# A two-layer decoder trunk on one core: TensorE's instructions in program order, paired values together

## The chip, the cores and the metric

The kernel runs on one core of one Trainium2 chip. The core has TensorE for matrix products (PE in the rows, and PEld for its weight loads), VectorE (DVE), ScalarE (ACT), GpSimd (POOL), and DMA queues that SyncE (SP) feeds. The metric is device time in microseconds, the median of several executions. One execution was profiled.

## The reference

Two layers work on x of 256 tokens and 1024 features in float32, with 256 tokens of memory. Each layer adds four parts to x:

```python
for layer in range(DEPTH):
    x = x + 0.5 * swiglu_ffn(rms_norm(x, ffn1_norm[layer]), ffn1_w_gu[layer], ffn1_w_down[layer])
    h = rms_norm(x, mix_norm[layer])
    if layer % 2 == 0:
        x = x + even_mixer(h, ...)      # sliding-window heads with sinks | stick-breaking heads
    else:
        x = x + odd_mixer(h, ...)       # 16 heads, a mixture of three dilated windows
    x = x + memory_cross_attention(rms_norm(x, xa_norm[layer]), rms_norm(mem, xa_mem_norm[layer]), ...)
    x = x + 0.5 * swiglu_ffn(rms_norm(x, ffn2_norm[layer]), ffn2_w_gu[layer], ffn2_w_down[layer])
```

The feed-forward has 2816 hidden features and is (silu(gate) * up) @ w_down. In the even mixer, 8 query heads share 2 key heads over a window of 128 tokens, and 8 more heads weigh by stick-breaking: the weight of a key is the exponential of log_sigmoid(z) plus the sum of log_sigmoid(-z) over the keys that come after it. Cross-attention has 4 heads of 256 features into the memory.

## The kernel before

Tokens are worked in two blocks t of 128. Each float32 product is made of three of a faster 32-bit type: a weight chunk is loaded (L170), rounded to a high half wh by ScalarE (L172), and the rest, wl, is made by VectorE (L174); activations are split in the same way (L187, L188). `mm3` (L179 to L181) then multiplies high by high, high by low and low by high into one PSUM bank. Feed-forwards use a wider form (L316, L317). Six PSUM banks named mm hold products, two named tp hold transpositions (L205, four blocks of 128 each, or L383). Ten work tiles wk, four raw buffers and ten weight pairs go round.

The order of the work around attention is written by a small planner in the kernel. `later(delay, fn, tag)` puts a step on a heap; each matmul group calls `tick(ns)`, which moves a made-up clock and runs a step that is due; `need(tag)` runs the rest of a tag at once. The delays stand in the table LAG. So the steps of attention are called between the matmuls of a projection. What is then issued first is not settled by that order alone: the framework's scheduler, on leaving the kernel, orders each engine's instructions by its own estimate of when they can start, and may pass a later one ahead. In a block under `tc.manual_schedule` an engine keeps the program's order; before, only the start of the first feed-forward (`start`) stands in one.

Both windowed attentions use `attend`. `one(i)` asks for scores of a head group (L594 in the even mixer, L827 in the odd one, each call for two groups at once), adds the bias (L601, L832), takes the maximum (L607, L837) and the exponential (L452). `share` divides by the sum (L438). `two` transposes the weights (L205), copies them to a work tile (L467) and asks for `values`, whose matmuls are on L482 by way of `value_pairs`. There are six groups in the even mixer's band part and twelve in the odd mixer.

The stick-breaking part (`stick`, from L680 on) makes scores for two heads at once (L691, L694), adds a mask (L699), takes an absolute value, an exponential and a logarithm on ScalarE (L702 to L704), and for each head VectorE and ScalarE make the high and low half of the log terms (L708, L710, L711). `after` sums them by three matmuls (L720, L721, L722), VectorE adds (L724), ScalarE takes the exponential (L725), and for every second head `values` follows. Beside it run the memory's keys (`mem.keys`, mm3, with squares on L511 and a scaling on L438).

In cross-attention, `attend` has its own form; its weights' transposition is asked for by `later(LAG['x_p'], turn, "o0")`.

Of the kernel before, what the change touches and what calls it, by code (L numbers as in the profile page):

```python
# [27 lines left out]


LAG = {  # L30
    "norm": 5000, "silu": 5000, "pv": 3000, "head256": 2200, "band": 7500, "band_gap": 2600, "band_p": 7500,
    "put": 400, "att_norm": 4500, "band_norm": 3500, "stick_gap": 1900, "stick_u": 3200, "stick_v": 1000, "stick_o": 1300, "head64": 7000,
    "att_first": 3800, "att_gap": 3300, "att_p": 17600, "att_o": 1800, "x_s": 18000, "x_p": 4000, "x_out": 3600,
    "mem_e": 5400, "mem_o": 4600, "rs64": 2700, "rs256": 1900, "rsband": 6100,
}

# [2 lines left out]
def kernel(  # L39
# [52 lines left out]
    def later(delay, fn, tag=None):  # L92
        serial[0] += 1
        heapq.heappush(heap, (clock[0] + delay, serial[0], tag, fn))
# [21 lines left out]
    plan = []  # L116
    for layer in range(DEPTH):
        plan += [(layer, 0, ffn1_norm), (layer, 1, mix_norm), (layer, 2, xa_norm), (layer, 3, ffn2_norm)]
    if phases is not None:
        plan = [plan[i] for i in phases]  # L120
# [30 lines left out]
    def slot(dt=F32):  # L151
        return big.tile([P, 1024], dt, name="big")

    def work(dt=F32):
        return wk.tile([P, 512], dt, name="wk")
# [30 lines left out]
    def split_to(dh, dl, src):  # L186
        nc.scalar.copy(dh, src)  # L187
        nc.vector.tensor_tensor(dl, src, f32(dh), op=ALU.subtract)  # L188
# [12 lines left out]
    def transpose4(src):  # L201

        ps = psum() if upcoming.get("starting") else tps()
        for b in range(4):
            nc.tensor.transpose(ps[:, b * P:(b + 1) * P], src[:, b * P:(b + 1) * P], ident)  # L205
        tick(440)
        return ps
# [51 lines left out]
    def project(view, lhs, evac, nk=NK, tags=(None, None)):  # L259

        head = nk - 8
        ps = [[None, None], [None, None]]

        def step(t, c, k, w):
            if k == 0:
                ps[t][c] = psum()
            mm3(ps[t][c], lhs(t, k), cols(w, c * 512, 512), k == 0, k == nk - 1)
            tick(650)

        for k in range(head):  # L270
            w = weights(view(k))
            for t in range(2):
                for c in range(2):
                    step(t, c, k, w)
        if tags[0]:
            need(tags[0])
        ws = []
        for k in range(head, nk):
            ws.append(weights(view(k)))
            for c in range(2):  # L280
                step(0, c, k, ws[-1])
        for c in range(2):
            evac(0, c, ps[0][c])
        if tags[1]:
            need(tags[1])
        for c in range(2):
            for k in range(head, nk):
                step(1, c, k, ws[k - head])
            evac(1, c, ps[1][c])
# [139 lines left out]
    def scale_heads(dst, src, r, n, pair=False):  # L429

        h = src.shape[1] // n
        if pair:
            nc.vector.tensor_tensor(
                dst.rearrange("p (b hf d) -> p hf b d", hf=2, d=n), src.rearrange("p (hf b d) -> p hf b d", hf=2, d=n),
                r[:, 0:h].rearrange("p (hf b) -> p hf b", hf=2).unsqueeze(3).broadcast_to([P, 2, h // 2, n]),
                op=ALU.mult)
        else:
            nc.vector.tensor_tensor(blocks(dst, n), blocks(src, n),  # L438
                                    r[:, 0:h].unsqueeze(2).broadcast_to([P, h, n]), op=ALU.mult)

    def attend(groups, scores, values, gap, norm, wait, first=0.0, tag=None, ready=None):

        def one(i):
            p, nm, sink = scores(groups[i])
            n, keys = p.shape[1], p.shape[2]
            dn = sm.tile([P, 4], F32, name="dn")  # L450
            for j in range(n):
                nc.scalar.activation(p[:, j, :], p[:, j, :], AF.Exp, bias=nm[:, j:j + 1], accum_out=dn[:, j:j + 1])  # L452
            p = p.rearrange("p a b -> p (a b)")
            if sink is not None:
                nc.scalar.activation(sink, sink, AF.Exp)

            def share():
                if sink is not None:
                    nc.vector.tensor_tensor(dn[:, 0:n], dn[:, 0:n], sink, op=ALU.add)
                nc.vector.reciprocal(dn[:, 0:n], dn[:, 0:n])  # L460
                scale_heads(p, p, dn, keys)
            later(norm, share, tag)

            def two():
                ps = transpose4(p)
                pt = work()
                nc.vector.tensor_copy(pt, ps)  # L467
                if ready is None:
                    later(LAG['pv'], lambda: values(groups[i], pt), tag)
                else:  # L470
                    ready(groups[i], lambda: later(LAG['pv'], lambda: values(groups[i], pt), tag))
            later(wait, two, tag)
            if i + 1 < len(groups):
                later(gap, lambda: one(i + 1), tag)
        later(first, lambda: one(0), tag)
# [395 lines left out]
    class Memory:  # L871
# [11 lines left out]
        def values(self, arrived):  # L883

            self.v = [(slot(F32R), slot(F32R)) for _ in range(2)]

            def evac(t, c, ps):
                split_to(*[d[:, c * 512:(c + 1) * 512] for d in self.v[t]], ps)
                if t == 1:
                    arrived(c)  # L890
            project(lambda k: self.w[k * P:(k + 1) * P, 1024:2048], self.parts, evac)

    def cross_attention(w_q, q_gain, k_gain, w_o, next_vec, mem):
# [55 lines left out]
        def evac(t, c, ps):  # L949
            norm_turn(t, c, ps)  # L950
            if c == 1:
                later(LAG['x_s'], lambda: attend(t, 0), "o0")
                later(LAG['x_s'] + 2000, lambda: attend(t, 1), "o0")
# [12 lines left out]
    neg_ur = const.tile([P, P], F32R, name="neg_ur")  # L966
    nc.vector.tensor_copy(neg_ur, neg_u)
    mems = [Memory(xa_w_kv[layer], xa_mem_norm[layer]) for layer in range(DEPTH)]
    for i, (layer, part, _) in enumerate(plan):
        j = layer // 2  # L970
        nxt = plan[i + 1][2][plan[i + 1][0]] if i + 1 < len(plan) else None
        mem = mems[layer]
        cross = (layer, 2) in [p[:2] for p in plan]
        if part == 0:
            ffn(ffn1_w_gu[layer], ffn1_w_down[layer], nxt, first=i == 0)
        elif part == 1 and layer % 2 == 0:
            even_mixer(ev_w_in[j], ev_q_gain[j], ev_k_gain[j], ev_sinks[j], ev_w_out[j], nxt, mem, first=i == 0)
        elif part == 1:
            odd_mixer(od_w_in[j], od_q_gain[j], od_k_gain[j], od_w_out[j], nxt, mem)
        elif part == 2:  # L980
            cross_attention(xa_w_q[layer], xa_q_gain[layer], xa_k_gain[layer], xa_w_o[layer], nxt, mem)
        else:
            ffn(ffn2_w_gu[layer], ffn2_w_down[layer], nxt)


def shape_constants():
# [53 lines left out]
```

## Time and profile before

| what | value |
|---|---|
| median of 3 runs | 1205.25 us (1201.16, 1205.25, 1205.61) |
| the profiled execution's own time | 1201.73 us |
| its span, first to last instruction | 1200.0 us |
| mean granted TensorE clock | 0.999 |
| TensorE busy | 1186.6 us, 99% of the span |
| TensorE weight loads busy | 997.0 us, 83% |
| VectorE busy | 774.3 us, 65% |
| ScalarE busy | 646.7 us, 54% |

A matmul's record lasts longer than the distance to the next one, so its busy time overlaps; distances between starts tell how fast the stream runs. The clock is given in shares of full speed.

### The profile page before, as it was taken

Reading aid. Unit: us, or ns where it says so; the run is one execution under the profiler, and the core shown is the slowest. Engines: PE = TensorE matmul, PEld = TensorE weight load, DVE = VectorE, ACT = ScalarE, POOL = GpSimd, SP = SyncE. Lnnn points to the kernel's source line nnn. Section 1 sums busy time; section 2 is a strip of 40 time slices with the busy share of each in tenths; the row PEclk is TensorE's granted clock in tenths of the full one; section 3 lists DMA queues with packets and bytes.
Section 4 is the critical chain, followed back from the end, with each engine's and each line's share of the span. In section 5 each row is a group of like instructions: output and inputs, shape, how many; then the busy total and the mean of one; then the engine's idle time right before and its main releaser. Section 6 shows DMA issues by size and latency. Waiting matters only on the chain.

```text
span 1200.0 us, 16955 instructions
## 1 busy us (share of the span) xinstructions
PE 1186.6 (99%) x6318; PEld 997.0 (83%) x6318; DVE 774.3 (65%) x1024; ACT 646.7 (54%) x1080; POOL 64.6 (5%) x123
## 2 busy tenths in 40 slices
PE   8999999999999999999999999999999999999998
PEld 6888888986788888888888888888777888888887
DVE  6766645696777666665375665376786676667651
ACT  6656534655665466555365564265763554655540
POOL 1000000200110000000000000032000100000000
PEclk9999999999999999999999999999999999999999
DMA  8865664731454485556385657445743645665550
GB/s 269 248 208 175 213 212 136 257 103 49 141 179 151 145 268 171 184 211 210 106 259 180 195 188 271 135 158 171 244 148 124 212 140 158 203 205 188 183 191 35
DMA packets 136756, 216.70 MB, mean 181 GB/s; under 512 B 10337, under 2 KB 104161, under 8 KB 136674
## 3 DMA queue, kind: packets, MB, share of 16 engines
q1 hardware_dynamic: 136674, 215.63, 55.1%
q8 instruction: 49, 0.80, 0.3%
q14 instruction: 33, 0.27, 0.1%
HBM read 214.54 MB, written 1.05 MB: 180 GB/s over the span
## 4 chain that ended last, share of the span: by engine, by line
PE 93%; DVE 3%; DMA 1%; ACT 1%; issue 1%; POOL 0%; SPq 0%; ACTq 0%; POOLq 0%; DVEq 0%
PE mm L316 23%; PE mm L179 18%; PE mm L181 18%; PE mm L180 18%; PE mm L317 12%; PE tp L205 3%; DVE wl L174 1%; PE mm L482 1%; DMA raw<-in_xa_w_o_dram 1%; PE mm L827 0%; PE mm L298 0%; DMA x<-in_x_dram 0%; ACT wh L172 0%; DVE big L188 0%; DMA raw<-in_ffn_w_gu_dram 0%
## 5 line engine op out<-in xcount | busy, mean ns | idle before, releaser
L174 DVE TENSOR_TENSOR wl<-raw,wh 128x1024 fp32r<-128x1024 f32 x386 | 463.8, 1220 | 144.7 <-ACT wh L172 142.5
L172 ACT CAST wh<-raw 128x1024 fp32r<-128x1024 f32 x386 | 394.2, 1051 | 156.0 <-PE mm L181 80.4
L316 PE MATMUL mm<-xs,wh 128*128 128x512 f32 x1184 | 413.7, 394 | 0.0
L317 PE MATMUL mm<-xs,wl 128*128 128x256 f32 x1184 | 331.8, 280 | 0.0
L316 PEld LDWEIGHTS mm<-xs,wh 128*128 128x128 f32 x1184 | 221.8, 187 | 50.4
L317 PEld LDWEIGHTS mm<-xs,wl 128*128 128x128 f32 x1184 | 223.8, 189 | 0.0
L179 PE MATMUL mm<-wh,big 128*128 128x512 f32 x480 | 191.5, 399 | 0.3 <-DVE wk L699 0.3
L180 PE MATMUL mm<-wl,big 128*128 128x512 f32 x480 | 188.3, 392 | 0.0
L181 PE MATMUL mm<-wh,big 128*128 128x512 f32 x480 | 188.3, 392 | 0.0
L179 PE MATMUL mm<-wh,xs 128*128 128x512 f32 (+1 forms) x432 | 171.8, 398 | 0.0
L181 PE MATMUL mm<-wh,xs 128*128 128x512 f32 (+1 forms) x432 | 167.1, 387 | 0.0
L180 PE MATMUL mm<-wl,xs 128*128 128x512 f32 (+1 forms) x432 | 167.0, 387 | 0.0
L320 ACT COPY wk<-mm 128x256 f32<-128x256 f32 x148 | 55.3, 374 | 147.7 <-PE mm L317 147.3
L321 DVE TENSOR_TENSOR wk<-mm,wk 128x256 f32<-128x256 f32 x148 | 62.2, 421 | 95.4 <-ACT wk L320 95.4
L179 PEld LDWEIGHTS mm<-wh,big 128*128 128x128 f32 x480 | 90.5, 188 | 20.1 <-issue 2.5
L181 PEld LDWEIGHTS mm<-wh,big 128*128 128x128 f32 x480 | 90.5, 189 | 19.5 <-issue 0.3
L180 PEld LDWEIGHTS mm<-wl,big 128*128 128x128 f32 x480 | 90.6, 189 | 17.5 <-issue 0.2
L181 PEld LDWEIGHTS mm<-wh,xs 128*128 128x128 f32 x432 | 81.1, 188 | 16.9 <-issue 0.2
L179 PEld LDWEIGHTS mm<-wh,xs 128*128 128x128 f32 x432 | 81.3, 188 | 15.0 <-issue 0.5
L180 PEld LDWEIGHTS mm<-wl,xs 128*128 128x128 f32 x432 | 81.4, 189 | 14.5 <-issue 0.2
L205 PE MATMUL tp<-ident,wk 128*128 128x128 f32 x352 | 52.8, 274 | 2.5 <-DVE big L188 0.8
L205 PEld LDWEIGHTS tp<-ident,wk 128*128 128x128 f32 x352 | 42.2, 140 | 14.2 <-issue 2.1
(144 smaller groups left out, 916.3 us busy)
## 6 DMA issues: line engine op xcount, KB each, us to landing
raw<-in_ffn_w_gu_dram SPq DMA_DIRECT2D x344, 256.0 KB, 4.2
raw<-in_ffn_w_down_dram SPq DMA_DIRECT2D x88, 512.0 KB, 4.3
raw<-in_xa_w_kv_dram SPq DMA_DIRECT2D x32, 512.0 KB, 5.4
raw<-in_od_w_in_dram SPq DMA_DIRECT2D x24, 512.0 KB, 4.3
raw<-in_ev_w_in_dram SPq DMA_DIRECT2D x18, 512.0 KB, 4.7
raw<-in_xa_w_q_dram SPq DMA_DIRECT2D x16, 512.0 KB, 4.2
raw<-in_xa_w_o_dram SPq DMA_DIRECT2D x16, 512.0 KB, 4.6
raw<-in_ev_w_out_dram SPq DMA_DIRECT2D x8, 512.0 KB, 3.8
```

The source lines that it names most:

```text
L172: nc.scalar.copy(wh, r)
L174: nc.vector.tensor_tensor(wl, r, f32(wh), op=ALU.subtract)
L179: nc.tensor.matmul(ps, lhsT=a[0], rhs=b[0], start=start, stop=False)
L180: nc.tensor.matmul(ps, lhsT=a[0], rhs=b[1], start=False, stop=False)
L181: nc.tensor.matmul(ps, lhsT=a[1], rhs=b[0], start=False, stop=stop)
L205: nc.tensor.transpose(ps[:, b * P:(b + 1) * P], src[:, b * P:(b + 1) * P], ident)
L316: nc.tensor.matmul(ps, lhsT=wh, rhs=xs[:, :, :, k, :], start=k == 0, stop=False)
L317: nc.tensor.matmul(ps[:, 0:256], lhsT=wl, rhs=xh[:, :, k, :], start=False, stop=k == NK - 1)
L320: nc.scalar.copy(part[:, bs], ps[:, 256:512])
L321: nc.vector.tensor_tensor(out[:, bs], ps[:, 0:256], part[:, bs], op=ALU.add)
L482: nc.tensor.matmul(dst(h)[rows], lhsT=lhs(h), rhs=rhs(h), start=first, stop=last)
```

## The change

The loop over the eight parts of the trunk is put under `tc.manual_schedule` for TensorE alone, so that from there on TensorE's instructions are issued in the order in which the program calls them. The other engines' orders are still the scheduler's. In `attend`, the values of a group wait for the next group's transposition, and both are then issued together. Three delays grow: silu from 5000 to 8000, pv from 3000 to 3500, x_p from 4000 to 5500.

```diff
 LAG = {
-    "norm": 5000, "silu": 5000, "pv": 3000, "head256": 2200, "band": 7500, "band_gap": 2600, "band_p": 7500,
+    "norm": 5000, "silu": 8000, "pv": 3500, "head256": 2200, "band": 7500, "band_gap": 2600, "band_p": 7500,
...
-    "att_first": 3800, "att_gap": 3300, "att_p": 17600, "att_o": 1800, "x_s": 18000, "x_p": 4000, "x_out": 3600,
+    "att_first": 3800, "att_gap": 3300, "att_p": 17600, "att_o": 1800, "x_s": 18000, "x_p": 5500, "x_out": 3600,
...
+        turned = []
+
         def one(i):
...
                 ps = transpose4(p)
                 pt = work()
                 nc.vector.tensor_copy(pt, ps)
+                turned.append((groups[i], pt))
+                if i % 2 == 0:
+                    return
+                both = turned[-2:]
+
+                def values_of_both():
+                    for g, weights_T in both:
+                        values(g, weights_T)
                 if ready is None:
-                    later(LAG['pv'], lambda: values(groups[i], pt), tag)
+                    later(LAG['pv'], values_of_both, tag)
                 else:
-                    ready(groups[i], lambda: later(LAG['pv'], lambda: values(groups[i], pt), tag))
+                    ready(groups[i], lambda: later(LAG['pv'], values_of_both, tag))
...
-    for i, (layer, part, _) in enumerate(plan):
-        j = layer // 2
+    with tc.manual_schedule(engines={mybir.EngineType.PE}):
+        for i, (layer, part, _) in enumerate(plan):
+            j = layer // 2
...
```

In the orders below, lines of the changed kernel are ten higher from the values on: L482 is L492, L691 and L694 are L701 and L704, L720 to L722 are L730 to L732. A name is result<-operands; tp and mm are the two kinds of PSUM bank, xs holds activations, wk work tiles.

TensorE at the end of the even mixer's band part, from the fifth group's transposition on. Before:

```order
L482 MATMUL mm<-wk,big 64x128
L205 MATMUL tp<-ident,wk 128x128 x4
L482 MATMUL mm<-wk,big 64x128 x3
L179 MATMUL mm<-wh,big 128x512
L180 MATMUL mm<-wl,big 128x512
L181 MATMUL mm<-wh,big 128x512
L691 MATMUL mm<-big 128x2x128 x2
L482 MATMUL mm<-wk,big 64x128 x4
L694 MATMUL mm<-big 128x128 x2
L205 MATMUL tp<-ident,wk 128x128 x4
```

The same place now:

```order
L205 MATMUL tp<-ident,wk 128x128 x8
L492 MATMUL mm<-wk,big 64x128 x8
L205 MATMUL tp<-ident,wk 128x128 x4
L492 MATMUL mm<-wk,big 64x128 x8
L179 MATMUL mm<-wh,big 128x512
L180 MATMUL mm<-wl,big 128x512
L181 MATMUL mm<-wh,big 128x512
L701 MATMUL mm<-big 128x2x128 x2
L704 MATMUL mm<-big 128x128 x2
```

The last transpositions and values of the band now follow each other with no key projection and no stick scores between them; the first stick scores come after all of them.

TensorE in the stick part, one step of sums with the next scores. Before:

```order
L720 MATMUL mm<-wk,neg_ur 128x384
L691 MATMUL mm<-big 128x2x128
L721 MATMUL mm<-wk,neg_ur 128x384
L722 MATMUL mm<-wk,neg_99 128x128
L691 MATMUL mm<-big 128x2x128
L694 MATMUL mm<-big 128x128 x2
```

The same step now (neg_ur and neg_99 are the constant matrices that sum over keys):

```order
L730 MATMUL mm<-wk,neg_ur 128x384
L731 MATMUL mm<-wk,neg_ur 128x384
L732 MATMUL mm<-wk,neg_99 128x128
L179 MATMUL mm<-wh,big 128x512
L180 MATMUL mm<-wl,big 128x512
L181 MATMUL mm<-wh,big 128x512
L701 MATMUL mm<-big 128x2x128 x2
L704 MATMUL mm<-big 128x128 x2
```

Sum and scores were laid into each other piece by piece; now each stands unbroken.

TensorE at the end of the odd mixer's attention. Before:

```order
L205 MATMUL tp<-ident,wk 128x128 x8
L482 MATMUL mm<-wk,big 64x128 x4
L205 MATMUL tp<-ident,wk 128x128 x4
L482 MATMUL mm<-wk,big 64x128 x8
L179 MATMUL mm<-wh,xs 128x512
L205 MATMUL tp<-ident,wk 128x128 x8
L180 MATMUL mm<-wl,xs 128x512
L181 MATMUL mm<-wh,xs 128x512
L179 MATMUL mm<-wh,xs 128x512
L180 MATMUL mm<-wl,xs 128x512
L181 MATMUL mm<-wh,xs 128x512
L482 MATMUL mm<-wk,big 64x128 x4
```

The same place now:

```order
L205 MATMUL tp<-ident,wk 128x128 x12
L492 MATMUL mm<-wk,big 64x128 x8
L205 MATMUL tp<-ident,wk 128x128 x8
L492 MATMUL mm<-wk,big 64x128 x8
L205 MATMUL tp<-ident,wk 128x128 x8
L492 MATMUL mm<-wk,big 64x128 x8
L179 MATMUL mm<-wh,xs 128x512
```

The matmuls of the output projection (those with xs) that stood between the last transpositions and values now come after all of them.

## Rows read from the trace of the kernel before

**Rows 1.** The page: busy time, share of the span and instructions of TensorE.

```profile
PE 1186.6 (99%) x6318; PEld 997.0 (83%) x6318; DVE 774.3 (65%) x1024; ACT 646.7 (54%) x1080; POOL 64.6 (5%) x123
```

**Rows 2.** Windows of 20 us: length, each engine's busy us, clock, DMA.

```profile
160.00:180.00 20.00, 20.00 (x90) 16.57 (x89) 8.58 (x7) 7.37 (x7) 0.00 (x0) 1.00 0.65 192
240.00:260.00 20.00, 19.25 (x164) 17.29 (x163) 19.73 (x46) 12.79 (x38) 0.00 (x0) 1.00 0.36 121
280.00:300.00 20.00, 18.32 (x78) 12.15 (x77) 10.65 (x21) 11.61 (x29) 2.04 (x4) 0.91 0.00 1
880.00:900.00 20.00, 19.60 (x123) 14.54 (x122) 16.23 (x28) 14.67 (x42) 2.91 (x7) 1.00 0.36 122
```

**Rows 3.** Timeline of TensorE, stick part: start, us, operation [idle before <-releaser].

```profile
263.31 0.70 PE L691 MATMUL mm<-big 64*128 64x256 f32 x4
...
264.53 0.49 PE L694 MATMUL mm<-big 64*128 64x128 f32 x4
...
275.06 0.38 PE L722 MATMUL mm<-wk,neg 128*128 128x128 f32 x2
...
282.57 0.34 PE L720 MATMUL mm<-wk,neg_ur 128*128 128x384 f32 x1
...
285.32 0.65 PE L482 MATMUL mm<-wk,big 128*64 128x256 f32 x2 [0.36 <-ACT wk L725]
286.87 0.45 PE L720 MATMUL mm<-wk,neg_ur 128*128 128x384 f32 x1 [0.90 <-ACT wk L710]
...
288.40 0.62 PE L179 MATMUL mm<-wh,big 128*128 128x512 f32 x1 [0.27 <-DVE wk L699]
...
298.74 0.39 PE L181 MATMUL mm<-wh,big 128*128 128x512 f32 x1
298.96 0.33 PE L720 MATMUL mm<-wk,neg_ur 128*128 128x384 f32 x1
...
299.45 0.47 PE L179 MATMUL mm<-wh,big 128*128 128x512 f32 x1
...
314.99 0.66 PE L205 MATMUL tp<-ident,wk 128*128 128x128 f32 x4
```

**Rows 4.** Lines, shapes apart: busy us, mean ns | idle before.

```profile
L174 DVE TENSOR_TENSOR wl<-raw,wh 128x1024 fp32r<-128x1024 f32 x386 | 463.8, 1220 | 144.7 <-ACT wh L172 142.5 <-PE mm L317 0.6
...
L467 DVE COPY wk<-tp 128x512 f32<-128x512 f32 x18 | 12.2, 682 | 1.3 <-PE tp L205 1.3
```

**Rows 5.** Timeline of VectorE, end of the odd mixer's attention.

```profile
906.15 1.28 DVE L467 COPY wk<-tp 128x512 f32<-128x512 f32 x2
```

**Rows 6.** Timeline of TensorE, band part of the even mixer.

```profile
249.14 0.60 PE L205 MATMUL tp<-ident,wk 128*128 128x128 f32 x4
...
251.92 0.66 PE L205 MATMUL tp<-ident,wk 128*128 128x128 f32 x4 [0.75 <-DVE big L188]
```

**Rows 7.** Timeline of VectorE, the first mask addition of the stick part.

```profile
268.63 1.01 DVE L699 TENSOR_TENSOR wk<-mm,smask 128x384 f32<-128x384 f32 x2
```

**Rows 8.** Timeline of TensorE, end of the odd mixer's attention.

```profile
886.87 0.60 PE L205 MATMUL tp<-ident,wk 128*128 128x128 f32 x4
...
899.81 0.65 PE L205 MATMUL tp<-ident,wk 128*128 128x128 f32 x4 [0.40 <-DVE wk L467]
...
901.61 0.66 PE L482 MATMUL mm<-wk,big 128*64 128x128 f32 x8 [0.56 <-DVE wk L467]
...
908.80 0.50 PE L181 MATMUL mm<-wh,xs 128*128 128x512 f32 x1
```

**Rows 9.** Timeline of TensorE, cross-attention of the second layer.

```profile
967.03 0.63 PE L205 MATMUL tp<-ident,wk 128*128 128x128 f32 x4 [0.71 <-DVE wk L438]
```

**Rows 10.** Timeline of TensorE, the first feed-forward's start.

```profile
14.30 0.28 PE L179 MATMUL mm<-xs,wh 128*128 128x256 f32 x1
14.42 0.28 PE L180 MATMUL mm<-xs,wh 128*128 128x256 f32 x1
14.97 0.74 PE L298 MATMUL mm<-xs,wl 128*128 128x256 f32 x4 [0.28 <-DVE wl L174]
```

More of the change, by code (lines that the diff above doesn't have):

```diff
@@ L968 @@
     mems = [Memory(xa_w_kv[layer], xa_mem_norm[layer]) for layer in range(DEPTH)]
-    for i, (layer, part, _) in enumerate(plan):
-        j = layer // 2
[L971 to L983, printed above, removed]
+    with tc.manual_schedule(engines={mybir.EngineType.PE}):
+        for i, (layer, part, _) in enumerate(plan):
+            j = layer // 2
+            nxt = plan[i + 1][2][plan[i + 1][0]] if i + 1 < len(plan) else None
+            mem = mems[layer]
+            cross = (layer, 2) in [p[:2] for p in plan]
+            if part == 0:
+                ffn(ffn1_w_gu[layer], ffn1_w_down[layer], nxt, first=i == 0)
+            elif part == 1 and layer % 2 == 0:
+                even_mixer(ev_w_in[j], ev_q_gain[j], ev_k_gain[j], ev_sinks[j], ev_w_out[j], nxt, mem, first=i == 0)
+            elif part == 1:
+                odd_mixer(od_w_in[j], od_q_gain[j], od_k_gain[j], od_w_out[j], nxt, mem)
+            elif part == 2:
+                cross_attention(xa_w_q[layer], xa_q_gain[layer], xa_k_gain[layer], xa_w_o[layer], nxt, mem)
+            else:
+                ffn(ffn2_w_gu[layer], ffn2_w_down[layer], nxt)
 def shape_constants():
```

## The prediction

> **What bounds the kernel now.** I read the page's busy shares first, then TensorE's windows of 20 us, then its timeline and VectorE's where a window is thin, and last the durations by line. The page puts TensorE at 1186.6 of 1200.0 us [rows 1], so by that row no order of the same matmuls can give back more than 13.4 us. The windows correct this. In 160 to 180 us, plain 512-column matmuls, the weight loads take 16.57 of 20 us at full clock; in 280 to 300 they take 12.15 though the matmuls still look 92% busy, and the granted clock is 0.91 [rows 2]. A matmul record overlaps the next, so a thin stretch hides in it.
>
> The Trainium skill says the same (page "Trainium Kernel Development and Optimization", section "Performance Expectations"): matmul busy time is a bad metric of distance to the roofline, weight-load busy share a good one. By it the window 280 to 300 alone lacks (16.57 - 12.15) / 16.57 of 20 us, an estimated 5.3 us, where the busy row lacks 1.68.
>
> So there are two thin places, both in attention: the even mixer's, from 240 to 315 us, and the odd mixer's, about 886 to 909. Elsewhere the stream is dense, and there the new order is the old one but for a few transpositions of the later feed-forwards that are asked for later; TensorE waits for none of them before, and I cost them at nothing, since only the much later down projection reads what they make. In the thin places VectorE sets the pace: it is busy 19.73 of 20 us from 240 to 260 and 16.23 from 880 to 900 [rows 2]. That is the heart of the case: an order on TensorE cannot make VectorE finish sooner; it only decides what TensorE does meanwhile.
>
> **The change part by part**, on the axis of the profiled execution, with these prices. A 512-column matmul every 0.22 us (298.74 to 298.96), which I take as 0.23; an unbroken sum of three lines (L720 to L722) in 0.49 (298.96 to 299.45); a pair of stick scores in 0.70 + 0.49 as recorded, 1.15 overlapped [rows 3]. VectorE's copies of 512 columns are recorded at 0.68, and two stand in 1.28, so 0.60 apart in a row, which I take for its other operations of that width too; a weight half (L174) takes 1.22 [rows 4, 5]. I add 0.1 us at each change between whole and half tiles.
>
> *Band attention, even mixer.* The transposition at 251.92 waits for VectorE to empty one of two banks; before, it waited 0.75 us, after 12 matmuls of 256 columns had filled the time since 249.14 [rows 6]. In the new order only three stand there. It still starts at 251.92, so it waits about 2.0 us, and nine matmuls, 1.1 us at 0.12, come later. The third pair of scores is that much later too. From then on I follow VectorE's own queue: two additions, two maxima, two shares, three copies at 0.60, one weight half at 1.13, and small ones for some 0.6, make 7.1 us from the scores' end near 257.2 to the share of the fifth group at 264.3. TensorE has run out at 262.2 and waits 2.1. The sixth transposition (0.35) and the last values behind its copy (0.65) wait as well, with nothing between, since the scheduler's fillers are gone. The stick scores, at 263.31 before [rows 3], now come at 269.5.
>
> *Stick part.* That is less bad than it looks. Before, the early scores lay until VectorE's addition at 268.63 [rows 7]; now the addition comes at 270.8. The first sum ends at 275.1 against 275.06 plus its last matmul [rows 3], after a wait of 0.4 for its low half. From there to the transposition at 314.99 before took 39.9 us [rows 3]. Its pieces were broken up: one sum and one pair of scores, 1.64 us unbroken, took from 282.57 to 285.32 less 0.36 of waiting, so 2.4 [rows 3]. After: 93 matmuls of 0.23 (21.4), three pairs of scores (3.5), seven sums (3.5), four sets of values at 1.1 (4.4), three transpositions (1.0), 16 changes of tile (1.8): 35.6. Waits that remain, by the queues of ScalarE and VectorE: the fifth sum behind the key squares (1.0), a key transposition behind the stick additions (0.6), the last sum (0.3), and the last values, whose exponential stands behind squares that need the six matmuls issued just ahead (1.4). Sum 38.9, end near 314.2. **Even mixer: -0.8 us.** Bounds: no wait at all is -0.8 - 3.3 - 5.1 = -9; all the broken pieces' gain lost (a further 3 us of waits) is about +2.5, more if the clock falls (below).
>
> *Odd mixer.* Six bursts of paired values instead of twelve save about 0.4 us by 886.87, where both orders stand alike [rows 8]. Then VectorE must do the same copies and shares; its last two copies were at 906.15 and ended at 907.43 [rows 5]. Before, the scheduler put eleven matmuls of the output projection between these transpositions and values, and TensorE waited visibly only 0.40 and 0.56; the matmul behind the last values began at 908.80 [rows 8]. In the new order the eleven follow all values. With VectorE freed of nothing I get its last copy near 906.5 (its first weight half comes 1.2 us earlier, a later wait eats some of that), TensorE waiting 0.7, 1.05, 0.45 and 0.9 on the way, the last values done at 907.1 and eleven matmuls (2.5) still owed. Against 908.80 that is **+1.0 us**; bounds -2.1 (none of the 3.1 us of waits) and +3 (VectorE no earlier at all, and a tail as before).
>
> *Cross-attention.* The probabilities' transposition at 967.03 waited 0.71 us for VectorE [rows 9]; it now stands six matmuls (1.4 us) later, behind what it waits for. The outputs come 3 instead of 9 matmuls after the last one, but start with the other half, whose pieces are then 2 us old. **-0.9 us**, bounds 0 and -1.1.
>
> *Start.* Two matmuls of 256 columns, 0.12 apart, that stood in a wait of TensorE are now behind it [rows 10]: **+0.2**, bounds 0 and +0.3.
>
> Sum: -0.8 + 1.0 - 0.9 + 0.2 = -0.5. The profiled execution took 1201.73 us, 1200.0 of them the span. The three runs give 1201.16, 1205.25 and 1205.61: it belongs to the lower level, and the median lies 3.5 above. The sum gives 1201.2 on the one and 1204.8 on the other level; I take the middle, **1203 us**.
>
> **The rivals.** *A: faster.* The waits that I drew are my weakest numbers. If ScalarE and VectorE keep ahead of the unbroken stick part (its 3.3 us go) and the waits of band (5.1) and odd tail (3.1) are half of mine, the sum is -0.5 - 3.3 - 2.6 - 1.5 = -7.9: 1194 to 1197. For it speaks that ScalarE worked only 11.61 of 20 us at 280 to 300 [rows 2], so the chain had room; against it, that the chain there is in series and that VectorE is full ahead of it.
>
> *B: slower, by the clock.* Before 288.40 TensorE waited 0.36, 0.90 and 0.27 us in a stretch of small pieces [rows 3], and then ran at the lower of the clock's two levels, 1.2 instead of 2.4 GHz: a granted 0.91 over 20 us is 3.6 us at half speed, 1.8 us lost [rows 2]. The matmul at 288.40 was recorded at 0.62 instead of 0.39 [rows 3]. The new order has five waits of 0.9 to 2.1 us with little between: 251.9, 264.3, 268, and two in the odd tail. If each is followed by such a fall, they cost 9.0, less the 1.8 of the one at 288 that then has no cause: -0.5 + 7.2 = +6.7, so 1208 to 1212. It decides from the fourth fall on; up to three fall within the forecast. Against it: around 899.81 and 901.61 TensorE waited twice with only transpositions and values between [rows 8], and no lower clock shows in 880 to 900.
>
> The Trainium skill (page "TensorE: Matmul & The Clock Gate", section "Part 1: The HAM clock gate") makes throttled the default state and activity what releases it. By that rule the emptier tails speak against this change; the trace agrees at 288 and has no counterpart at 900.
>
> *C: nothing happens.* Outside the thin places the scheduler's order was the program's already. If the even and odd terms cancel as drawn, the change does what it says and moves no time; this is the forecast's middle and not a separate case.
>
> **How the numbers follow.** A measurement of this kernel tells some 0.5%, 6 us, from no change. Forecast (1198 to 1209 over both levels): 0.54. A: 0.28. B: 0.18. Part of each rival lies inside 0.5%, and part of the forecast's edge outside, about equally, so faster 0.28, same 0.54, slower 0.18. The range, 1194 to 1211, takes in all of the forecast, most of A at either level and half of B.
>
> **What would show it.** Right: TensorE waits about 2 us near 252 and near 264, and stick sums that stand unbroken, some 4 us apart between pairs, the marked transposition at 314 to 315; in the odd tail waits that add to about 3 us and the output projection's first matmul near 907; no wait of a transposition near 967. Wrong: if the transposition now at 314.99 comes before 311, VectorE and ScalarE had more room than I gave them; if it comes after 317 or the clock row falls below 1.00 at 250 to 270 or 900 to 910, rival B.

## The result, and the profile after

The changed kernel took 1210.11 us (median of 5 runs, 1207.82 to 1213.23), the kernel before 1202.54 (5 runs beside it): ratio 1.0054, interval 1.0036 to 1.0073. By the medians it is slower by 7.6 us, by the ratio by some 6.5, where the sum forecast 0.5 less; 1210 lies inside the range, and the direction is wrong. Its first profiled execution took 1213.23 us, 1211.5 of them the span.

Its page, TensorE's busy line and the costliest of its matmul groups (busy us, mean ns of one | idle before):

```profile
PE 1189.2 (98%) x6318; PEld 1000.8 (83%) x6318; DVE 774.7 (64%) x1024; ACT 647.4 (53%) x1080; POOL 63.2 (5%) x123
L316 PE MATMUL mm<-xs,wh 128*128 128x512 f32 x1184 | 418.9, 399 | 0.0
```

The same group on the page of before:

```profile
L316 PE MATMUL mm<-xs,wh 128*128 128x512 f32 x1184 | 413.7, 394 | 0.0
```

The busy line is [rows 1] over again: 2.6 us more for TensorE's matmuls and 3.8 for its weight loads, and next to nothing for the other engines. The second row is the one to stop at: the same 1184 matmuls, in the feed-forwards, where I looked for nothing, last 5 ns longer each. Windows of 20 us of the changed kernel (columns as in [rows 2]):

```profile
240.00:260.00 20.00, 18.15 (x145) 17.19 (x144) 17.91 (x38) 11.35 (x33) 0.00 (x0) 0.91 0.47 159
260.00:280.00 20.00, 17.59 (x129) 13.42 (x127) 16.65 (x35) 12.04 (x28) 0.00 (x0) 0.91 0.32 105
280.00:300.00 20.00, 19.32 (x106) 14.25 (x105) 13.34 (x27) 13.88 (x34) 2.03 (x4) 1.00 0.00 1
480.00:500.00 20.00, 20.00 (x115) 17.32 (x114) 14.20 (x19) 10.89 (x17) 0.00 (x0) 1.00 0.61 187
900.00:920.00 20.00, 17.18 (x136) 12.96 (x135) 19.29 (x29) 11.66 (x23) 0.93 (x2) 1.00 0.44 128
```

And the fourth of them in the kernel before:

```profile
480.00:500.00 20.00, 20.00 (x117) 17.62 (x117) 12.51 (x18) 11.75 (x18) 0.00 (x0) 1.00 0.56 178
```

At 480 both are 100% busy at full clock, yet 115 matmuls start instead of 117, and weight loads fill 17.32 instead of 17.62 us. This is the wide stretch of a feed-forward (L316 and L317, 512 and 256 columns by turns). TensorE's timeline there, before:

```profile
484.79 0.39 PE L316 MATMUL mm<-xs,wh 128*128 128x512 f32 x1
485.02 0.28 PE L317 MATMUL mm<-xs,wl 128*128 128x256 f32 x1
485.13 0.39 PE L316 MATMUL mm<-xs,wh 128*128 128x512 f32 x1
...
485.83 0.39 PE L316 MATMUL mm<-xs,wh 128*128 128x512 f32 x1
```

and after, with one of the two places where the silu step's transpositions (L383) are laid into the stretch:

```profile
454.90 0.28 PE L317 MATMUL mm<-xs,wl 128*128 128x256 f32 x1
455.02 0.38 PE L383 MATMUL tp<-ident,wk 128*128 128x128 f32 x2
455.16 0.48 PE L316 MATMUL mm<-xs,wh 128*128 128x512 f32 x1
...
489.52 0.40 PE L316 MATMUL mm<-xs,wh 128*128 128x512 f32 x1
489.75 0.28 PE L317 MATMUL mm<-xs,wl 128*128 128x256 f32 x1
489.87 0.40 PE L316 MATMUL mm<-xs,wh 128*128 128x512 f32 x1
...
490.58 0.40 PE L316 MATMUL mm<-xs,wh 128*128 128x512 f32 x1
```

Three pairs take 1.04 us before (484.79 to 485.83) and 1.06 after (489.52 to 490.58), with no gap in either: 346.7 and 353.3 ns a pair. I call them the fast and the slow gait. They change where transpositions interrupt the stretch. Before, each of the last three stretches has 15 pairs at the slow pace, an interruption, and 273 pairs at the fast pace; after, it has two interruptions, after 9 and after 24 pairs, and the 264 pairs behind the second are slow. The first feed-forward is slow in both.

Both kernels issue 6318 matmuls, so the distance between matmuls of the same number tells where time went. From the first profile of each, in us (rows with ' are second and third profiled executions, told of below):

| kernel | start to first wide matmul | to second wide stretch (even mixer in it) | 2nd, 3rd, 4th wide stretch | third to fourth (odd mixer in it) |
|---|---|---|---|---|
| before | 24.91 | 304.12 | 99.90, 99.90, 99.90 | 309.97 |
| before' | 27.23 | 305.10 | 101.63, 99.90, 99.90 | 309.79 |
| after | 28.08 | 305.63 | 101.74, 101.74, 101.69 | 311.52 |
| after' | 24.95 | 305.08 | 101.74, 101.69, 101.74 | 312.84 |
| after'' | 26.55 | 303.76 | 101.74, 101.74, 101.74 | 311.16 |

The rest agrees within 0.2 us. So the first pair of profiles differs by 3.2 at the start, 1.5 with the even mixer, 5.5 by the gait and 1.6 with the odd mixer.

The rows of TensorE's timeline after that answer to [rows 3, 6, 8, 9]; a row stands 3.2 us later than its place on the axis of before in the even mixer, and 8.3 later in the odd one:

```profile
255.11 0.68 PE L205 MATMUL tp<-ident,wk 128*128 128x128 f32 x4 [1.85 <-DVE big L188]
...
268.95 0.81 PE L205 MATMUL tp<-ident,wk 128*128 128x128 f32 x4 [2.14 <-DVE dn L461]
...
274.98 0.70 PE L701 MATMUL mm<-big 64*128 64x256 f32 x4
...
305.11 0.65 PE L205 MATMUL tp<-ident,wk 128*128 128x128 f32 x4 [1.61 <-DVE wk L438]
...
315.24 0.86 PE L492 MATMUL mm<-wk,big 128*64 128x256 f32 x6 [1.44 <-ACT wk L735]
...
319.98 0.60 PE L205 MATMUL tp<-ident,wk 128*128 128x128 f32 x4
...
899.15 0.66 PE L205 MATMUL tp<-ident,wk 128*128 128x128 f32 x4 [1.18 <-DVE wk L469]
...
911.39 1.06 PE L205 MATMUL tp<-ident,wk 128*128 128x128 f32 x8 [1.53 <-DVE wk L438]
...
915.57 1.26 PE L492 MATMUL mm<-wk,big 128*64 128x128 f32 x16 [0.65 <-DVE wk L469]
916.76 0.50 PE L179 MATMUL mm<-wh,xs 128*128 128x512 f32 x1
...
977.99 0.60 PE L205 MATMUL tp<-ident,wk 128*128 128x128 f32 x4
```

The waits stand near where they were forecast, and the one of cross-attention is gone. What the sum did not have is the clock's 0.91 in both windows from 240 to 280, the sign that the prediction had named for rival B: it falls behind the waits of 1.85 and 2.14 us. The fall that the kernel before has at 280 to 300 [rows 2] is gone in turn, so the changed kernel has one more here, not two.

### The profile page after: what moved, and what is told of

It is laid out like the page before. It is cut to its first block, busy times and chain, and to the rows that moved or that the text cites. A ratio compares the mean times of both kernels' runs of the same rounds, so it can differ in the third digit from the quotient of the medians.

```text
span 1211.5 us, 16957 instructions
## 1 busy us (share of the span) xinstructions
PE 1189.2 (98%) x6318; PEld 1000.8 (83%) x6318; DVE 774.7 (64%) x1024; ACT 647.4 (53%) x1080; POOL 63.2 (5%) x123
## 4 chain that ended last, share of the span: by engine, by line
PE 89%; DVE 5%; ACT 2%; DMA 2%; issue 1%; SPq 0%; POOL 0%; ACTq 0%; DVEq 0%; POOLq 0%
PE mm L316 23%; PE mm L179 17%; PE mm L180 17%; PE mm L181 17%; PE mm L317 12%; PE tp L205 2%; DVE wl L174 2%; PE mm L298 1%; PE mm L492 1%; ACT wh L172 1%; DMA wk<-in_dil_bias_dram 0%; DMA x<-in_x_dram 0%; DVE wk L469 0%; DVE wk L438 0%; DMA raw<-in_ev_w_out_dram 0%
## 5 line engine op out<-in xcount | busy, mean ns | idle before, releaser
L316 PE MATMUL mm<-xs,wh 128*128 128x512 f32 x1184 | 418.9, 399 | 0.0
L317 PE MATMUL mm<-xs,wl 128*128 128x256 f32 x1184 | 332.5, 281 | 0.0
L316 PEld LDWEIGHTS mm<-xs,wh 128*128 128x128 f32 x1184 | 222.4, 188 | 54.9
L317 PEld LDWEIGHTS mm<-xs,wl 128*128 128x128 f32 x1184 | 223.7, 189 | 0.1
```

Of the source, the lines that this page charges most:

```text
L316: nc.tensor.matmul(ps, lhsT=wh, rhs=xs[:, :, :, k, :], start=k == 0, stop=False)
L317: nc.tensor.matmul(ps[:, 0:256], lhsT=wl, rhs=xh[:, :, k, :], start=False, stop=k == NK - 1)
```

## The experiments

**Is the silu delay the cause of the gait?** Undone in the changed kernel, and made alone in the kernel before:

```diff
-    "norm": 5000, "silu": 8000, ...      # a: the changed kernel
+    "norm": 5000, "silu": 5000, ...
-    "norm": 5000, "silu": 5000, ...      # b: the kernel before
+    "norm": 5000, "silu": 8000, ...
```

> The changed kernel with the delay silu put back from 8000 to 5000. Theory G (gait): in the feed-forwards' wide stretch (L316, L317) one pair of matmuls comes every 346.7 or every 353.3 ns, and each pair of transpositions that is laid into the stretch turns the one into the other. The kernel before has one such interruption in each of the last three feed-forwards and then runs at 346.7; the changed one has two and runs at 353.3, about 245 pairs by 6.6 ns, 1.6 us a time, 4.9 us in all. By G this kernel runs at 346.7 in all three and is 4.9 us faster than the changed one, 2.7 us over the kernel before, near 1205. Rival W (the 7.6 us are waits in the mixers and at the start): no change of pace, near 1210.

Measured: 1207.04 us (ratio to before 1.0033, 1.0021 to 1.0045); the stretches take 99.90 us, all three.

> The kernel before with the delay silu at 8000 and nothing else. Theory G: two interruptions in each of the three wide stretches, pairs at 353.3 ns after them, 4.9 us slower than the kernel before, near 1207.4. Rival W: these transpositions are awaited by nobody, so no change, 1202 to 1203.

Measured: 1208.34 us against 1203.21 (1.0046, 1.0034 to 1.0058); the stretches take 101.74. The window of 480 to 500 us, of a and then of b:

```profile
480.00:500.00 20.00, 20.00 (x118) 17.62 (x117) 13.55 (x20) 10.65 (x19) 0.00 (x0) 1.00 0.68 210
```

```profile
480.00:500.00 20.00, 20.00 (x115) 17.33 (x114) 12.08 (x19) 10.30 (x18) 0.00 (x0) 1.00 0.66 208
```

One number that moves a few transpositions, which nobody waits for, so that two pairs of them instead of one stand in each wide stretch, costs the kernel before 5.1 us: G holds and W falls. In the changed kernel it gave back 3.1 by the medians and 5.5 by the stretches. With the further profiled executions below, the spans differ by 5 us in the mean (three of the changed kernel, two of this one).

**The order alone, and the rest alone.**

```diff
+    with tc.manual_schedule(engines={mybir.EngineType.PE}):   # the kernel before, nothing else
...
-    with tc.manual_schedule(engines={mybir.EngineType.PE}):   # the changed kernel, silu 5000
```

> The kernel before with TensorE in program order and nothing else (old delays, values not paired). Theory G: pairs at 346.7 ns in the last three feed-forwards; what is lost is lost in the mixers, and more than in the changed kernel since each group's values wait for their own copy: even mixer +2 to +4, odd +2 to +4, start +0.2, so 1206 to 1210. Rival W: as slow as the changed kernel or slower, 1210 or more, since the order is the cause of all of it.

Measured: 1213.35 us (1.0089, 1.0069 to 1.0108). All three stretches fast; the way from third to fourth stretch takes 318.32 us, 8.4 more than before, where 2 to 4 were expected; the way with the even mixer takes 1.5 more. So the time is rival W's, but its fast stretches speak against W: the order alone leaves their pace as it was and loses in the mixers. In the odd one values wait for their own copies, three times, and the clock is down for a part of it. The longest item of TensorE's waits from 885 to 925 us, and the window from 890 to 930 (TensorE's busy time and count, clock, DMA):

```profile
PE mm L482 <- DVE wk L467: 4.4, 3, 1.6
```

```profile
890.00:930.00 40.00, 33.96 (x201) 0.91 0.32 112
```

With the values paired (and pv and x_p longer), the same list of the changed kernel (below) has 0.8 us for them: it is the pairing, by these waits, that made the order bearable in the odd mixer.

> The changed kernel without the block of program order and with silu at 5000: paired values, pv 3500 and x_p 5500 alone, TensorE's order left to the scheduler. Theory G: pairs at 346.7 ns, cross-attention keeps its 1.2 us (both layers), the mixers come out as in the kernel before within 1 us: 1200 to 1203. Rival P (the pairing of values itself costs the mixers' time, not the order): even and odd mixer lose 2 us each also here, 1204 to 1206.

Measured: 1203.48 us (1.0001, 0.9990 to 1.0011). The second layer's cross-attention keeps 0.8; the odd mixer takes 3.1 more than before, with a clock of 0.96 from 890 to 930, which is some 1.6 of them; the even mixer is unchanged. So without order and silu the change is worth nothing. P falls for the even mixer; for the odd one it rests on this one profiled execution, the slowest of the twelve (1205.96), and is not shown.

**Does an odd count of interruptions bring the fast gait back?** A pair of unread transpositions in each of the last three stretches of the changed kernel (a_third):

```diff
+            if not first and c == 4:
+                pst = tps()
+                for b in range(2):
+                    nc.tensor.transpose(pst[:, b * P:(b + 1) * P], f32(hts[0][0][:, b * P:(b + 1) * P]), ident)
```

> The changed kernel (silu 8000) with a third interruption, a pair of transpositions that nobody reads, laid into each of the last three wide stretches after its 96th pair. Theory G: an odd count of interruptions brings the pairs back to 346.7 ns for the last 190 or so: 1.25 us less the 0.4 of the interruption, three times, -2.5 us against the changed kernel, near 1207.5. Rival S (the later place of the silu transpositions in itself costs, by what they make VectorE or ScalarE do late): pairs stay at 353.3, +1.2 us, near 1211.

Measured: 1207.45 us (1.0039, 1.0026 to 1.0052), and each stretch 100.70 instead of 101.74. Windows ahead of and behind the third interruption:

```profile
455.00:475.00 20.00, 20.00 (x115) 17.37 (x114) 14.60 (x20) 12.64 (x20) 0.00 (x0) 1.00 0.52 161
490.00:510.00 20.00, 20.00 (x117) 17.66 (x116) 14.33 (x20) 12.07 (x19) 0.00 (x0) 1.00 0.61 184
```

The median's 2.7 us against the changed kernel lie within what the two intervals leave open, but each stretch is 1.04 us shorter with two transpositions more in it, and the windows show the gait change at the interruption: S falls.

**Can the first stretch be turned?** The same pair after 32 pairs of the first stretch, and x_p 5500, in the kernel before.

```diff
+            if first and c == 1:
+                pst = tps()
...
-    "x_p": 4000
+    "x_p": 5500
```

> The kernel before with two edits: a pair of transpositions whose result nobody reads is laid into the wide stretch of the first feed-forward (after its 32nd pair), and x_p is 5500. Theory G (gait): the first feed-forward ran at 353.3 ns a pair in every kernel so far, with no interruption in it; after this one it runs at 346.7, some 285 pairs by 6.67 ns, 1.9 us less the 0.4 that the interruption takes; x_p gives 0.8 in the second layer and 0.1 in the first (the segments of the kernel without program order). Together -2.4 us: near 1200.6. Rival L (the pace of the first feed-forward is set by its own loads or operands, not by what went before): its pairs stay at 353.3, the dummy costs 0.4, total -0.5.

Measured: 1201.76 us (0.9987, 0.9977 to 0.9997). The first stretch stays slow (112.93 us); x_p gives its 0.8. By itself this speaks for L. Two explorations followed, both in the changed kernel with silu 5000: other kinds of interruption (a_kinds), then pairs at other distances (a_phase).

```diff
+    cuts = [{1: [('T', 1)], 2: [('T', 1)], 3: [('T', 2)], ...},      # one list for each feed-forward
+            {3: [(512, 1)], 4: [(512, 1)], 5: [(256, 1)], ...}, ...]
```

> The changed kernel with silu at 5000 and, at the end of chunks of the wide stretches, different interruptions whose result nobody reads. First feed-forward: 1, 1, 2, 2, 3, 3, 4, 4 and 2 transpositions of 128 columns. Second: one matmul of 512 columns twice, of 256 twice, of 128 twice, then a transposition. Third: two matmuls of 128 twice, of 256 twice, of 512 twice, then a transposition. Fourth: 1, 1, 2, 1, 3, 3, 4 transpositions. Theory G as the runs so far show it knows only pairs of transpositions, which turn 353.3 into 346.7 ns and back. G1 (any interruption turns the gait): it changes at each. G2 (the count of instructions decides): odd and even counts differ, 1 and 3 do one thing, 2 and 4 another. G3 (columns decide, by the time they shift): 512 columns, in whatever form, behave alike. The time itself says little: plus some 4 us of interruptions.

Measured: 1214.29 us in the one run. The first eight interruptions of the first stretch left it slow, whatever they were. The ninth turned it. In the other stretches a pair of transpositions turned the gait each of four times, one transposition never of five, and three transpositions or plain matmuls by no rule that I can see: G1, G2 and G3 as stated all fall.

```diff
+                if pairs[0] in (30, 61, 93, 123, 154, 186, 216, 249, 282):      # in ws_wide
+                    d = tps()
+                    for i in range(2):
+                        nc.tensor.transpose(...)
```

> The changed kernel with silu at 5000 and with pairs of unread transpositions in the first wide stretch alone, after its pairs 30, 61, 93, 123, 154, 186, 216, 249 and 282, so at distances 30, 31, 32, 30, 31, 32, 30, 33 and 33. Theory G3 (place in the cycle of three pairs): the first cut turns the pace from 353.3 to 346.7 ns, the second turns it back, and from then on slow stretches turn where the distance is a multiple of three. Rival L (this first stretch has a cause of its own): 353.3 throughout, whatever the distance. The time: plus some 3 us of interruptions, less what fast pieces give.

Measured: 1211.54 us in the one run. The first stretch does turn: slow, slow, fast, slow, fast, slow, slow, fast, slow, fast. So L falls as well, and so does the rule of three (an interruption after 30 pairs turned it twice and failed once, one after 31 turned it). Over all profiles a pair of transpositions turned the gait 80 times of 88; five of the eight failures were in the first stretch, three where a stretch had begun fast and was only 9 pairs old. What decides in the failures stays open.

**Does the clock cost the even mixer its time?** Eight unread matmuls ahead of each of the two long waits of the band part, in the changed kernel with silu 5000 (a_fill):

```diff
+        if turns[0] - 1 in (14, 18):
+            idle = psum()
+            for _ in range(8):
+                nc.tensor.matmul(idle, lhsT=neg_ur, rhs=xh[:, 0, 0:4, :], start=True, stop=True)
```

> The changed kernel with silu at 5000, and with eight matmuls of 512 columns that nobody reads (1.8 us) ahead of the two transpositions for which TensorE waited 1.82 and 2.13 us in the band part. Theory K (clock): the even mixer's loss (1.7 us up to the key projection) is what the two half-clock stretches behind those waits cost; with TensorE busy through the waits both go, the even mixer comes to within 0.5 us of the kernel before, and the time is 1205.3. Rival V (VectorE): the band is VectorE's, the clock costs nothing on top; the waits are filled, the even mixer stays at +1.7 and the time at 1207, or a little more where the fill is longer than the wait.

Measured: 1204.85 us (1.0014, 1.0003 to 1.0024). Its windows, and its timeline at the filled waits:

```profile
240.00:260.00 20.00, 19.79 (x161) 17.69 (x159) 18.94 (x41) 12.52 (x38) 0.00 (x0) 1.00 0.49 159
260.00:280.00 20.00, 17.51 (x131) 13.57 (x129) 16.92 (x34) 12.02 (x25) 0.00 (x0) 1.00 0.34 106
```

```profile
252.66 1.97 PE L208 MATMUL mm<-xs,neg_ur 128*128 128x512 f32 x8
254.77 0.66 PE L211 MATMUL tp<-ident,wk 128*128 128x128 f32 x4
...
264.97 2.10 PE L208 MATMUL mm<-xs,neg_ur 128*128 128x512 f32 x8
267.53 0.63 PE L211 MATMUL tp<-ident,wk 128*128 128x128 f32 x4 [0.45 <-DVE dn L467]
```

The clock stays at 1.00, and from the band to the key projection the loss is 0.0 us instead of 1.7, though TensorE does 16 matmuls more. K holds, V falls. Two further kernels with these fills (a_early and the same with a filled start, below) also have the clock at 1.00 there and stand at +0.6 and +0.4; all eight profiled executions of this order without fills have one fall or two. But the kernel before has one as well [rows 2], and with one fall the unfilled order does no worse than the filled one (-0.5 to +0.1, below). So a wait of 2 us costs little by itself while VectorE is the pace; the second fall of the clock costs some 1.6 us.

The Trainium skill (page "TensorE: Matmul & The Clock Gate", section "Part 1: The HAM clock gate") calls the throttled state the default, which activity releases. This pair of runs agrees: the same place at 0.91 and at 1.00, by matmuls alone.

**Does the odd mixer lose its time in the bare tail?** Two delays of a_fill made shorter (a_early):

```diff
-    "att_gap": 3300, "att_p": 17600
+    "att_gap": 2900, "att_p": 11000
```

> The kernel with the filled band waits (changed kernel, silu 5000) and with the odd mixer's attention asked for earlier: att_p 11000 instead of 17600, att_gap 2900 instead of 3300, so that four groups instead of six are left for the bare tail of transpositions and values. Theory T (bare tail): the odd mixer's +2.2 to +3.8 us up to the output projection is VectorE's copies and shares in a tail with no matmuls beside them; with two groups fewer in it the odd mixer comes out 1.5 to 2.5 us earlier than in the kernel with the filled band, and no half-clock stretch falls in it: near 1203. Rival V (VectorE is the odd mixer's bound for the whole stretch from 880 on, wherever the steps stand): within 0.5 us of it, 1204.9.

Measured: 1206.00 us (1.0027, 1.0013 to 1.0040), no better than a_fill and above both forecasts. The clock is 1.00 throughout, the tail is two groups shorter, and the odd mixer is at +1.8. In the profiled execution of a_fill it was at +3.9, so T's 2 us are there; but that execution had a clock of 0.96 from 890 to 930, which is some 1.6 us, and the medians show no gain. TensorE's waits from 885 to 920 us (us in total, times, longest):

```profile
PE mm L498 <- DVE wk L475: 2.1, 1, 2.1
PE tp L211 <- DVE wk L444: 1.3, 1, 1.3
PE tp L211 <- DVE wk L475: 0.9, 1, 0.9
```

The same list of the changed kernel, 890 to 920:

```profile
PE tp L205 <- DVE wk L438: 1.8, 2, 1.5
PE tp L205 <- DVE wk L469: 1.6, 2, 1.2
PE mm L492 <- DVE wk L469: 0.8, 2, 0.6
```

4.3 us of waits against 4.2: they moved and did not shrink. T is not borne out; V is what is left, by exclusion only, since no run here made VectorE's part shorter.

**A version that beats both.** The kernel before with three edits: small matmuls that fill TensorE's waits at the start, x_p 5500, and an interruption after the first stretch's 30th pair.

```diff
+            warm(4)        # unread matmuls of a constant; then 3 and 2 more
...
+                if pairs[0] in (30,):
...
-    "x_p": 4000
+    "x_p": 5500
```

> The kernel before with three edits. One: while TensorE waits at the start for x (up to 2.5 us, then 0.4 to 1.9 more), it runs 4, 3 and 2 small matmuls of a constant that nobody reads. Two: x_p 5500. Three: the pair of transpositions in the first wide stretch stands after its 30th pair, no longer its 32nd. Theory K (clock): the profiles so far have the full clock granted from 12 to 20 us after the start, most of them from 18 on, and the first wide matmul at 24.9 where it came at 12.1, at 26.6 to 28.2 where it came at 18 to 20; with TensorE busy from 1.4 us on the clock comes by 12 and the wide stretch starts near 25, 2 us earlier than mostly. x_p gives 1.0 in all as measured. Theory G3 (what an interruption does depends on where in the slow gait's cycle of three pairs it falls: after 15 and 72 pairs, multiples of three, it turned to fast, after 32 it did not): 30 is a multiple of three, so the first wide stretch turns to 346.7 ns, -1.9 us. Together near -4.5: 1198.4. If G3 is wrong, -2.6: 1200.3; if K is wrong too, 1201.9.

Measured: 1199.51 us against 1202.51 (0.9972, 0.9961 to 0.9982), the fastest here: 0.3% under the kernel before, and 10.6 us under the changed kernel by the medians. The clock is full from 12 us on and the first wide matmul comes at 25.85. Only two profiled executions have the filled start (full clock from 12.0 and 10.5 us); in the sixteen without it, it came between 11.1 and 20.1, so what the fills give is not shown apart. The first stretch is fast:

```profile
60.00:80.00 20.00, 20.00 (x117) 17.62 (x116) 13.60 (x20) 10.65 (x19) 0.00 (x0) 1.00 0.68 210
1080.00:1100.00 20.00, 20.00 (x115) 17.39 (x114) 12.97 (x19) 10.29 (x18) 0.00 (x0) 1.00 0.67 211
```

The last stretch was slow in this execution, though its order is that of before: it entered fast, and the interruption turned it. The start's fills and the interruption on a_early instead:

> The same kernel as a_early with the filled start and with the pair of unread transpositions after the 30th pair of the first wide stretch. From the segments measured: start -1.0 to -2, first wide stretch -1.7, even mixer with cross-attention -0.5 to -0.8. Theory T: odd mixer with cross-attention at about 0, so 1199 to 1200, level with the best kernel in the scheduler's order (1199.5). Rival V: odd mixer with cross-attention +1.5 to +3, 1201 to 1203.

Measured: 1204.46 us (1.0015, 1.0001 to 1.0028), above both ranges. The way with the odd mixer is 2.7 longer than before, as V had it. The odd mixer alone is at +3.3, and it was at +1.8 in a_early, in the same order and both times at a clock of 1.00; what makes that difference is open. TensorE in program order did not reach the scheduler's order in any form tried.

**Program or execution?** Four more profiled executions: two of the changed kernel, one of the kernel before, one of the changed kernel with silu 5000.

> A second look at the changed kernel. If the pace belongs to the program (theory G), all of the last three wide stretches end at 353.3 ns a pair, as in the first look. If it belongs to the execution (theory X), at least one of the three ends at 346.7, and the time is about 1.6 us less for each. The band's two half-clock stretches come again near 255 and 269 us by theory K.

> A third look at the changed kernel, with the same expectations: G three stretches at 353.3 ns, X one or more of the six in the two looks at 346.7; K two half-clock stretches in the band.

> A second look at the kernel before. Theory G: the last three wide stretches at 346.7 ns a pair again; X: one or more at 353.3. The first wide matmul stood at 24.9 us in the first look and at 26.6 to 28.2 in most others: if that was luck, it stands at 26 or later here; and one half-clock stretch near 288 to 291 us, as in the first look.

> A second look at the changed kernel with silu at 5000. G: three stretches at 346.7 ns; X: one or more at 353.3, which would say why its median lay 3.1 us under the changed kernel's and not 5.2. K: two half-clock stretches in the band.

Measured: 1210.92, 1209.52, 1206.53 and 1204.56 us. The gait is nearly the program's: nine of nine stretches slow in the changed kernel, six of six fast with silu 5000, five of six fast before. Over all kernels with one pair of transpositions in each of the last three stretches, 30 of 36 had the fast gait behind it; the other six had all been entered in the fast gait, and the pair turned them. So it is the gait in which a stretch is entered that belongs to the execution. The start is chance: 24.95 and 26.55 us in the changed kernel, 27.23 before. And the band's clock falls once or twice in the same order. The third profiled execution of the changed kernel:

```profile
240.00:260.00 20.00, 18.10 (x153) 16.43 (x152) 18.99 (x41) 12.18 (x38) 0.00 (x0) 1.00 0.40 139
260.00:280.00 20.00, 17.61 (x124) 13.43 (x123) 16.75 (x35) 12.57 (x27) 0.00 (x0) 0.91 0.34 106
```

From the band to the key projection, against before: +1.8, +1.7 and +0.9 us in the three executions with two falls, -0.4 and -0.5 in the two with one. Three kernels above whose edits touch the feed-forwards alone carry the same order: +1.1 (a_third) and +1.0 (a_kinds) with two falls, +0.1 (a_phase) with one.

## Why the prediction was wrong

**The step that failed** is the sentence on the rest of the trunk: "a few transpositions of the later feed-forwards that are asked for later; TensorE waits for none of them before, and I cost them at nothing". That nobody waits for them is true. What they cost is the pace of what they interrupt: 264 pairs by 6.6 ns, three times, 5.2 of the 5.5 us by which the three stretches grew; b_silu8 measured 5.1 for that edit alone. It is most of the 7.6. With the means of the five profiled executions of this order (+0.7 in the even mixer, +2.2 in the odd one, -0.4 in the second layer's cross-attention) the 5.5 make 8.0. The rows to see it by were in the trace: the wide stretches of the kernel before ran at two paces, 353.3 in the first feed-forward and 346.7 in the others, and I had called them dense and alike.

**Even mixer, -0.8.** The waits came as drawn: 1.85 and 2.14 us at 251.9 and 265.8 on the axis of before (forecast 2.0 and 2.1, near 252 and 264). The marked transposition came at 316.8 instead of 314.2. By the executions with one clock fall it would be 314.5, and the term -0.4 to -0.5; with two falls +0.9 to +1.8. The mean of the five is +0.7. So this term came out near but for rival B's mechanism, which I had and priced at 1.8 a fall; its point of decision, four falls, was not reached, since the odd mixer had none or one.

**Odd mixer, +1.0.** Measured +2.2, +2.6 and +1.5. The waits add to 4.2 instead of 3.1; the excess is the 1.18 at 899.15, a transposition that waits for one of VectorE's copies, ahead of the tail that I had drawn. The first matmul of the output projection came at 908.5 (916.76 less 8.3), not 907.1. The mechanism was right and the size was not. (The recorded terms, 907.1 and 2.5 against 908.80, also add up to +0.8 and not to +1.0; little hangs on it.)

**Cross-attention, -0.9.** Right for the second layer: no wait near 967, and -0.9 there in every profiled execution with x_p 5500 but one (-0.4), though up to 0.5 came back before the next wide stretch. **Start, +0.2.** Not to be told from the 3 us by which starts differ.

**The levels.** I took the profiled 1201.73 for the lower of two levels. Some 80 executions of the kernel before lie between 1199.9 and 1208.1 us, thickest near 1202.5 and without a gap where I had put one. Its two profiled executions differ by the start (24.9 and 27.2), by a stretch's gait (1.7) and by 1.0 on the way with the even mixer.

**The rivals.** A (the waits are half of mine) fell: band, stick part and odd tail have 12.0 us of waits where I had drawn 11.5. B gave the right direction and 1208 to 1212 held the time, but by another mechanism for most of it; so it is luck that the range held 1210, since its upper end stood there for the clock. None of the three cases had the gait, so 0.18 for slower was too low for a reason that no re-weighing of the cases would have mended.

## What to carry to other kernels

A dense stretch at 100% busy and full clock can still have two paces: compare the count of matmuls, or of weight-load time, in equal windows of the same kind before calling a stretch alike, and cost a moved instruction by what it interrupts as well as by who waits for it. Where an engine must wait anyway, unread work in the wait can pay, where it spares a fall of the clock behind the wait. An order fixed by hand needs the fillers put in by hand too; here the scheduler's order kept them for free.

## What the runs showed of the hardware that I had not expected

The two gaits. In both, the engine shows no idle time and a granted clock of 1.00: 230 and 117 ns from one start to the next in the fast one; in the slow one a cycle of three pairs, 232, 118, 241, 120, 235 and 114 ns, that repeats without change for 264 or 320 pairs. A pair of transpositions turned one into the other 80 times of 88. Why there are two, and what decides in the other eight, is open.

The Trainium skill (page "TensorE: Matmul & The Clock Gate", section "Wait — 56ns, not 53.3ns?") gives one distance for back-to-back matmuls of N columns at full clock, N divided by 2.4 GHz plus about 2.5 ns; an estimate from it for a pair of 512 and 256 columns is 325 ns. The trace has 346.7 and 353.3, each matmul with weights of its own, and the measurement decides.

In the kernels without fills at the start the full clock was first granted between 11.1 and 20.1 us, and the first wide matmul moved with it from 24.9 to 28.2: a spread of 3 us, larger than any term of the sum.
